# A layer with three branches: first loads, turns, gate chain and pools in another order

## The chip, the core and the metric

The kernel runs on one core of a Trainium2 chip. Its engines each work through a queue of their own in order and wait for one another by semaphores: TensorE (PE) multiplies and transposes, VectorE (DVE) and ScalarE (ACT) do arithmetic and empty PE's result banks, GpSimd (POOL) does small things, SyncE (SP) issues DMA transfers. The metric is the time on the device in microseconds, the median of the runs.

## The reference

One decoder layer on 1024 tokens of width 1024, all in float32. Here only its first part matters:

```
h    = rms_norm(x)                 # then one input projection, cut into the branches
mkv  = rms_norm(mem) @ w_kv        # memory: 256 tokens
C:   qh = rms_norm(q per head);  mk = rms_norm(k part of mkv);  mv = v part
     y2 = softmax(qh mk^T * s) @ mv
A:   mLSTM over chunks of 128 tokens, 4 heads: running maximum m of the gates,
     decays exp(i - b - m), state C carried from chunk to chunk
gates = sigmoid(h @ w_gate + b);   merge, projections, MLP
```

Branch B (differential attention), the merge and the MLP follow and are not touched.

## The kernel before

Float32 products are made of three matmuls (`mm3`, L91): each operand is split into a high part, rounded by ACT (L111 or L114), and a low part, the remainder, by DVE (L112 or L115). A weight goes by DMA into a `raw` tile, is split into a `w` tile, and the `raw` tile is free for the next load when both are done. Tiles come from pools with a number of buffers per name; a pool that closes gives its memory to the next one, and a tile that lies where an old one lay waits for that one's last reader, a store among them.

PE writes into PSUM banks: `mm` for products, two `tp` banks in turn for transposes and small products, two `sc` tiles of two banks each. A bank is taken again only when its last contents have been read.

`consts` loads a table `vraw` and `lamv`, turns the table on PE (L192) and copies it to `vec` (L194), from which scales of the rows are read. `phase_x` loads the memory rows `mx`, squares and scales them (`norm_rows`, L231 to L233), and runs `mem_kv`, a generator: turn `mx` into `memT` (L243), scaled by `vec` while it is split, then project it with three groups of weights `wkv`: the keys (copied to `kr` at L266, normalised, turned into `mkT`), then the values `mv` in two groups. Between these it loads the rows `xk` of x, normalises and turns them into `hT`.

`branch_c` puts items at places in a stream of matmuls (`weave`): at each place of the stream the items due run. A place is three matmuls. Items are `turn` (queries `cqr` into `cqT`), `scores` (with exponentials `cpe` at L380, their sum, and scalings at L387), `ptr` (turn the probabilities `cpe` into `cpT`), `values` (product with `mv` into `yc`, stored to y2).

`branch_m` does the same for the mLSTM with a stream of its own. `m_gates` (place 66) computes the gate chain, with four round trips through DRAM; `m_gates2` turns its three rows `g_b`, `g_w`, `g_a` into columns `g_col` (L559, L561). For each of eight half heads: `inter` (broadcast load `wib`, its product with the queries, split into `qp`), `krows` (keys times a column, `ks`), `decays` (broadcast load `ngb`, mask, exponentials with a column), `scores` (into a `tp` bank, times `ngb`, split into `mpT`), four `chunk`s and `final`. Gate products fill the rest of the stream (`gates`). Behind it comes a stretch of gate products alone with pools `wpg` and `rpg`.

Of the kernel before, what the change touches and what calls it, by code (L numbers as in the profile page):

```python
# [10 lines left out]
F32 = mybir.dt.float32  # L11
F32R = mybir.dt.float32r
AF = mybir.ActivationFunctionType
# [4 lines left out]
P = 128  # L18
D = 1024
S = 1024  # L20
NT = 8
# [7 lines left out]
R_SUB, R_CQ, R_CK, R_DQ, R_DK, R_END = 96, 97, 98, 99, 100, 101  # L29
# [42 lines left out]
class Layer:  # L72
# [109 lines left out]
    def consts(self, tmp):  # L182
# [6 lines left out]
        nc.vector.memset(raw, 0.0)  # L189
        nc.sync.dma_start(raw[0:R_END, :], a["vecs"])  # L190
        ps = self.tp_tile()
# [23 lines left out]
        lv = tmp.tile([P, 256], F32, name="lamv")  # L215
        nc.sync.dma_start(lv, a["lamv"].partition_broadcast(P))
        pr = tmp.tile([P, 128], F32, name="lamp")
# [18 lines left out]
    def mem_kv(self, pool, tmp, xs):  # L236
        nc, a = self.nc, self.a
        memT = tmp.tile([P, NK, 2, 256], F32R, tag="memT", name="memT")
        for k in range(0, NK, 2):
            ps = self.tp_tile()  # L240
            for i in range(2):
                for t in range(2):
                    nc.tensor.transpose(  # L243
                        ps[:, (i * 2 + t) * P : (i * 2 + t + 1) * P], xs[t][:, (k + i) * P : (k + i + 1) * P], self.ident
                    )
            for i in range(2):
                self.split(
                    memT[:, k + i, 0], memT[:, k + i, 1], ps[:, i * 256 : (i + 1) * 256],
                    self.vec[:, R_MEM + k + i : R_MEM + k + i + 1],
                )  # L250
# [10 lines left out]

        w = self.load_w(a["wkv"][0], 512, 2)
        for t in range(2):
            ps = proj(w, t)
            kr = tmp.tile([P, 512], F32, tag="kr", name=self.name("kr"))
            nc.scalar.copy(kr, ps)  # L266
            scr = tmp.tile([P, D], F32, tag="sq", name=self.name("scr"))
            nc.scalar.activation(scr[:, 0:512], ps, AF.Square)
            r4 = tmp.tile([P, 4], F32, tag="r4", name=self.name("r4"))
            nc.vector.tensor_reduce(r4, scr[:, 0:512].rearrange("p (h d) -> p h d", h=4), axis=AX.X, op=ALU.add)  # L270
            self.rsqrt_mean(r4, r4, 128, 4)
            for h in range(4):
                nc.vector.tensor_scalar_mul(kr[:, h * P : (h + 1) * P], kr[:, h * P : (h + 1) * P], r4[:, h : h + 1])
            pt = self.tp_tile()
            for h in range(4):
                nc.tensor.transpose(pt[:, h * P : (h + 1) * P], kr[:, h * P : (h + 1) * P], self.ident)
            p4 = pt.rearrange("p (h t) -> p h t", h=4)
            self.split(self.mkT[:, :, 0, t * P : (t + 1) * P], self.mkT[:, :, 1, t * P : (t + 1) * P], p4)
        for g in range(2):
            w = self.load_w(a["wkv"][1 + g], 512, 2)  # L280
            yield
            for t in range(2):
                ps = proj(w, t)
                s = slice(g * 512, (g + 1) * 512)
                self.split(self.mv[:, t, 0, s], self.mv[:, t, 1, s], ps)

    def phase_x(self, kv, tmp):
# [13 lines left out]
        mem = [load(a["mem"][t * P : (t + 1) * P, :], "mx") for t in range(2)]  # L301
        for x in mem:
            norm(x)
        gen = self.mem_kv(kv, tmp, mem)
        next(gen)
        xs = [load(a["x"][t * P : (t + 1) * P, :], "xk") for t in range(NT)]

# [22 lines left out]
    def branch_c(self, pool):  # L330
# [67 lines left out]

        def values(hf, h, v):
            c = h * 256 + v * P  # L400
            ps = self.sc_tile()[:, 0:512]
            for j in range(2):
                self.mm3(
                    ps, (self.mv[:, j, 0, c : c + P], self.mv[:, j, 1, c : c + P]),
                    (pT[hf, h, j][:, 0], pT[hf, h, j][:, 1]), j == 0, j == 1,
                )
            y = pool.tile([P, 512], F32, tag="y", name=self.name("yc"))
            if v == 0:
                nc.scalar.copy(y, ps)
            else:  # L410
                V.tensor_copy(y, ps)
            self.store_y(2, h * 2 + v, hf, y)

# [5 lines left out]
        for hf in range(2):  # L419
            for h in range(4):  # L420
                b = (43, 78)[hf] + (4, 5)[hf] * h
                add(b, ptr, hf, h, 0)
                add(b + 1, ptr, hf, h, 1)
                add(b + 5, values, hf, h, 0)
                add(b + 5, values, hf, h, 1)
        self.weave(stream(), items)
# [136 lines left out]
    def branch_m(self, pool, gp, tail):  # L563
# [262 lines left out]
        for n in range(8):  # L826
            hd, hf = heads[n // 2], n % 2
            e = Epos[n]
            late = n == 0
            kt, st, ch, fi = (9, 2, 14, 34) if n == 0 else (-2, 2, 7, 33) if n == 1 else (-16, -8, 3, 29)  # L830
# [764 lines left out]
    def run(self):  # L1595
        tc, nc = self.tc, self.nc
        with ExitStack() as ctx:
# [22 lines left out]
            with ExitStack() as c1:  # L1620
# [6 lines left out]
                with ExitStack() as c2:  # L1627
                    E2 = lambda *x, **k: c2.enter_context(tc.tile_pool(*x, **k))
                    kv = E2(name="kv", bufs=1)
                    self.wp = E2(name="wp", bufs=4)  # L1630
                    self.rp = E2(name="rp", bufs=3)
                    with tc.tile_pool(name="ptmp", bufs=1) as tmp0, tc.tile_pool(name="ptmp2", bufs=2) as tmp, tc.tile_pool(name="ptmp8", bufs=8) as tmp8:
                        class T:
                            def tile(_, shape, dt, tag, name):
                                p = tmp8 if tag == "xk" else tmp if tag in ("mx", "sq", "r1", "r4") else tmp0
# [3 lines left out]
                    with tc.tile_pool(name="pc", bufs=2) as pc, tc.tile_pool(name="pc1", bufs=1) as pc1, tc.tile_pool(name="pc3", bufs=3) as pc3, tc.tile_pool(name="pc4", bufs=6) as pc4, tc.tile_pool(name="wpc", bufs=8) as self.gwp, tc.tile_pool(name="rpc", bufs=2) as self.grp:  # L1639
                        class T2:  # L1640
# [4 lines left out]
                        self.branch_c(T2())  # L1645
                with tc.tile_pool(name="wpm", bufs=25) as self.wp, tc.tile_pool(name="rpm", bufs=3) as self.rp, tc.tile_pool(name="gm", bufs=1) as gm, tc.tile_pool(name="pm1", bufs=1) as pm1, tc.tile_pool(name="pm", bufs=2) as pm, tc.tile_pool(name="pm3", bufs=3) as pm3:
                    class T3:
# [96 lines left out]
```

## Time and profile before

| | us |
|---|---|
| median of 3 runs | 2291.28 |
| lowest, highest | 2290.56, 2292.64 |
| span of the profiled execution | 2287.7 |
| median less that span | 3.6 |
| PE busy | 2203.0 (96%) |
| DVE, ACT, POOL busy | 1388.2, 1012.3, 543.9 |

All times in the rows below are microseconds from the start of the span. "Idle before" in brackets is how long an engine had done nothing, and behind the arrow stands what released it. PEclk is TensorE's granted clock, 1.00 for 2.4 GHz and 0.50 for 1.2 GHz. The span has four parts that matter here: the loads and the memory (0 to 66 us), branch C (66 to 183), the mLSTM (183 to 561), and the rest.

### The profile page before, as it was taken

Reading aid. Unit: us, or ns where it says so; the run is one execution under the profiler, and the core shown is the slowest. Engines: PE = TensorE matmul, PEld = TensorE weight load, DVE = VectorE, ACT = ScalarE, POOL = GpSimd, SP = SyncE. Lnnn points to the kernel's source line nnn. Section 1 sums busy time; section 2 is a strip of 40 time slices with the busy share of each in tenths; the row PEclk is TensorE's granted clock in tenths of the full one; section 3 lists DMA queues with packets and bytes.
Section 4 is the critical chain, followed back from the end, with each engine's and each line's share of the span. In section 5 each row is a group of like instructions: output and inputs, shape, how many; then the busy total and the mean of one; then the engine's idle time right before and its main releaser. Section 6 shows DMA issues by size and latency. Waiting matters only on the chain.

```text
span 2287.7 us, 30578 instructions
## 1 busy us (share of the span) xinstructions
PE 2203.0 (96%) x11222; PEld 1884.3 (82%) x11222; DVE 1388.2 (61%) x2627; ACT 1012.3 (44%) x1994; POOL 543.9 (24%) x696
## 2 busy tenths in 40 slices
PE   7999999999999999999899999999999999899998
PEld 5788789888898999999787888887787888688777
DVE  6636457552147777777652123454598777856678
ACT  6533445543246666666453112223445444543332
POOL 2100000000011111111000002201576665565553
PEclk9999999999999999999999999999999999999999
DMA  6023212201311110011134225435525444844434
GB/s 242 19 79 102 88 44 83 83 24 62 98 58 33 38 37 24 19 38 33 42 113 168 101 90 174 134 115 173 195 99 204 152 153 148 319 164 152 139 128 166
DMA packets 113781, 247.90 MB, mean 108 GB/s; under 512 B 11065, under 2 KB 19550, under 8 KB 111582
## 3 DMA queue, kind: packets, MB, share of 16 engines
q1 hardware_dynamic: 111326, 233.36, 30.4%
q10 hardware_dynamic: 2304, 12.58, 1.3%
q8 instruction: 88, 1.44, 0.3%
q14 instruction: 63, 0.52, 0.1%
HBM read 178.76 MB, written 67.14 MB: 107 GB/s over the span
## 4 chain that ended last, share of the span: by engine, by line
PE 70%; DVE 14%; DMA 7%; ACT 5%; issue 3%; POOL 2%; SPq 0%; ACTq 0%; DVEq 0%; POOLq 0%
PE mm L91 43%; PE p L91 18%; PE sc L91 4%; ACT dpe L987 2%; PE po L91 2%; DVE sc L979 1%; PE tp L94 1%; DMA wraw<-in_wdown 1%; DMA raw<-in_wd 1%; DVE wo L105 1%; DVE w L112 1%; DVE dpe L1000 1%; DVE daT L112 1%; DVE dq L867 1%; DMA raw<-in_wgate 1%
## 5 line engine op out<-in xcount | busy, mean ns | idle before, releaser
L91 PE MATMUL mm<-w,hT 128*128 128x384 f32 (+3 forms) x2496 | 474.0, 331 | 13.7 <-DVE dq L867 9.0
L91 PE MATMUL mm<-hT,w 128*128 128x512 f32 x1920 | 471.0, 400 | 8.2 <-ACT w L111 5.2
L91 PEld LDWEIGHTS mm<-hT,w 128*128 128x128 f32 x1920 | 360.1, 191 | 84.9 <-ACT w L111 5.8
L91 PEld LDWEIGHTS mm<-w,hT 128*128 128x128 f32 x2496 | 387.4, 189 | 33.3 <-DVE dq L867 13.7
L91 PE MATMUL p<-xd,wo 128*128 128x512 f32 x1344 | 314.1, 395 | 16.2 <-DVE acc L1543 8.5
L91 PEld LDWEIGHTS p<-xd,wo 128*128 128x128 f32 x1344 | 253.9, 190 | 76.3 <-DVE acc L1543 12.4
L91 PE MATMUL p<-xo,wo 128*128 128x512 f32 x1344 | 307.5, 390 | 3.2 <-DVE st L1397 1.8
L91 PEld LDWEIGHTS p<-xo,wo 128*128 128x128 f32 x1344 | 251.4, 188 | 57.9 <-ACT pt L1210 2.2
L112 DVE TENSOR_TENSOR w<-raw,w 128x256 fp32r<-128x256 f32 (+3 forms) x304 | 172.9, 589 | 162.4 <-ACT w L111 161.2
L91 PE MATMUL mm<-kt,w 128*128 128x512 f32 x1152 | 261.3, 389 | 0.0
L91 PEld LDWEIGHTS mm<-kt,w 128*128 128x128 f32 x1152 | 216.2, 188 | 45.0 <-DVE w L112 0.2
L111 ACT CAST w<-raw 128x256 fp32r<-128x256 f32 (+3 forms) x304 | 154.3, 532 | 193.5 <-PE mm L91 112.8
L104 ACT CAST wo<-wraw 128x896 fp32r<-128x896 f32 x122 | 114.8, 942 | 187.7 <-PE p L91 121.9
L105 DVE TENSOR_TENSOR wo<-wraw,wo 128x896 fp32r<-128x896 f32 x122 | 146.2, 1213 | 51.3 <-ACT wo L104 51.1
L1124 POOL TENSOR_TENSOR wraw<-wraw 128x128 f32<-128x128 f32 x128 | 100.9, 788 | 207.3 <-DMA wraw<-in_wdown 132.5
L987 ACT ACTIVATE dpe<-sc,dst,drr 128x256 f32<-128x256 f32 (+7 forms) x128 | 106.6, 833 | 94.0 <-DVE dst L983 92.0
L105 DVE TENSOR_TENSOR xd<-xd 128x1536 fp32r<-128x1536 f32 (+2 forms) x36 | 69.2, 1929 | 69.4 <-ACT xd L104 69.3
L979 DVE CUSTOM_DVE_ANT_0 sc<-sc,tmask 128x256 f32<-128x256 f32 (+7 forms) x128 | 96.9, 757 | 16.5 <-PE sc L91 16.5
L1125 POOL TENSOR_TENSOR wraw<-wraw 128x128 f32<-128x128 f32 x128 | 100.9, 788 | 0.0
L127 POOL TENSOR_SCALAR drr<-drr 128x16 f32<-128x16 f32 x16 | 3.6, 222 | 397.4 <-DVE drr L935 397.4
L1126 POOL TENSOR_TENSOR wraw<-wraw 128x128 f32<-128x128 f32 x128 | 90.7, 708 | 0.0
L127 POOL TENSOR_SCALAR hss<-hss 128x4 f32<-128x4 f32 x8 | 3.3, 409 | 356.2 <-ACT mscr L747 237.6
(319 smaller groups left out, 3084.9 us busy)
## 6 DMA issues: line engine op xcount, KB each, us to landing
wraw<-in_wup SPq DMA_DIRECT2D x64, 256.0 KB, 3.1
r_d<-xts SPq DMA_DIRECT2D x16, 1024.0 KB, 4.2
wraw<-in_wdown SPq DMA_DIRECT2D x64, 256.0 KB, 2.8
xd<-r_d SPq DMA_DIRECT2D x19, 768.0 KB, 6.9
xd<-r_d SPq DMA_DIRECT2D x14, 1024.0 KB, 5.9
raw<-in_wgate SPq DMA_DIRECT2D x48, 256.0 KB, 2.8
gates<-gt SPq DMA_DIRECT2D x48, 256.0 KB, 2.0
raw<-in_wd SPq DMA_DIRECT2D x32, 384.0 KB, 3.2
```

What stands on the lines that cost most here:

```text
L91: self.pin(self.nc.tensor.matmul(out, l, r, start=start, stop=stop))
L94: self.pin(self.nc.tensor.transpose(out, x, self.ident))
L104: self.A.copy(hi, src)
L105: self.V.tensor_sub(lo, src, f32(hi))
L111: nc.scalar.copy(hi, src)
L112: nc.vector.tensor_sub(lo, src, f32(hi))
L867: V.scalar_tensor_tensor(out=qT[lo, c], in0=pt[lo], scalar=self.gd[lo], in1=f32(qT[lo, c]), op0=ALU.mult, op1=ALU.subtract)
L979: V.tensor_tensor_reduce(out=sc[:, 0:n], in0=sc[:, 0:n], in1=self.tmask[:, D - n : D], scale=1.0, scalar=-3.0e38, op0=ALU.add, op1=ALU.max ...
L987: nc.scalar.activation(pe[c][:, 0:n], sc[:, 0:n], AF.Exp, bias=t8[:, 2 + c : 3 + c], scale=rr[:, i, c : c + 1], accum_out=t8[:, 4 + c : 5 ...
L1124: G.tensor_add(r[:, 4], r[:, 0], r[:, 3])
L1125: G.tensor_sub(r[:, 5], r[:, 4], r[:, 1])
L1126: G.tensor_sub(r[:, 6], r[:, 1], r[:, 0])
```

## The change

Seven edits. (1) `lamv` and `vraw` are loaded from ACT's queue instead of SP's. (2) The memory rows are turned as they are; the reciprocal root `rm` of their mean square is worked out beside it and multiplied in when `kr`, its squares and `mv` leave the bank. The first weights are requested before the turns, four rows of x before the second group's weights and four behind; `wp` has 5 buffers for 4, `rp` 4 for 3. (3) In branch C the turns of the probabilities stand three places later and four apart, the two halves of `values` become one item with one `sc` tile, one place later; `cpT` has 4 buffers for 3. (4) In the mLSTM `m_gates2` goes from 104 to 107, and for the first half head `krows`, `decays`, `scores`, the chunks and `final` go 2 to 5 places later; `inter` stays. (5) The pools of the mLSTM open in another order. (6) The scratch memory for DMA is 1024 instead of its default, so that more is left for tiles. (7) With that the places of later pools shift.

```diff
@@ consts
-        nc.sync.dma_start(raw[0:R_END, :], a["vecs"])
+        nc.scalar.dma_start(raw[0:R_END, :], a["vecs"])
...
-        nc.sync.dma_start(lv, a["lamv"].partition_broadcast(P))
+        nc.scalar.dma_start(lv, a["lamv"].partition_broadcast(P))
@@ mem_kv
+        w = self.load_w(a["wkv"][0], 512, 2)
+        yield
...
-        w = self.load_w(a["wkv"][0], 512, 2)
+        rm = []
+        for x in xs:
+            rm.append(tmp.tile([P, 1], F32, tag="rm", name=self.name("rm")))
+            scr = tmp.tile([P, D], F32, tag="sq", name=self.name("scr"))
+            nc.scalar.activation(scr, x, AF.Square, accum_out=rm[-1])
+            self.rsqrt_mean(rm[-1], rm[-1], D, 1)
...
-            nc.scalar.copy(kr, ps)
+            nc.scalar.activation(kr, ps, AF.Copy, scale=rm[t])
...
-            nc.scalar.activation(scr[:, 0:512], ps, AF.Square)
+            nc.scalar.activation(scr[:, 0:512], ps, AF.Square, scale=rm[t])
...
-                self.split(self.mv[:, t, 0, s], self.mv[:, t, 1, s], ps)
+                self.split(self.mv[:, t, 0, s], self.mv[:, t, 1, s], ps, rm[t])
@@ phase_x
-        for x in mem:
-            norm(x)
         gen = self.mem_kv(kv, tmp, mem)
         next(gen)
-        xs = [load(a["x"][t * P : (t + 1) * P, :], "xk") for t in range(NT)]
+        xs = [load(a["x"][t * P : (t + 1) * P, :], "xk") for t in range(4)]
+        next(gen)
+        xs += [load(a["x"][t * P : (t + 1) * P, :], "xk") for t in range(4, NT)]
@@ branch_c
-        def values(hf, h, v):
+        def values(hf, h):
+            sc = self.sc_tile()
+            for v in range(2):
...
-                b = (43, 78)[hf] + (4, 5)[hf] * h
+                b = (46, 79)[hf] + 4 * h
                 add(b, ptr, hf, h, 0)
                 add(b + 1, ptr, hf, h, 1)
-                add(b + 5, values, hf, h, 0)
-                add(b + 5, values, hf, h, 1)
+                add(b + 6, values, hf, h)
@@ branch_m
-        add(96 + 8, self.m_gates2, gp)
+        add(96 + 11, self.m_gates2, gp)
...
-            kt, st, ch, fi = (9, 2, 14, 34) if n == 0 else ...
+            kt, st, ch, fi = (12, 2, 19, 39) if n == 0 else ...
...
                 add(e + 9, inter, hd, hf)
-                add(e + 9, decays, hd, hf)
-                st = 10
+                add(e + 11, decays, hd, hf)
+                st = 13
@@ pools
-   wp 4, rp 3; pc3 3;  wpm 25, rpm 3, gm 1, pm1 1, pm 2, pm3 3
+   wp 5, rp 4; pc3 4;  gm 1, pm3 3, rpm 3, wpm 25, pm1 1, pm 2
-    nc = bacc.Bacc("TRN2", target_bir_lowering=False, num_devices=1)
+    nc = bacc.Bacc("TRN2", target_bir_lowering=False, num_devices=1, dynamic_dma_scratch_size=1024)
```

PE's order in branch C around the fifth scores (`sc<-mkT,cqT`): a `tp` row is one of the four transposes of a turn, of queries (`cqr`) or probabilities (`cpe`). Before, up to the scores:

```order
L94 MATMUL tp_967<-ident,cpe_735 128x128
L94 MATMUL tp_967<-ident,cpe_802 128x128
L94 MATMUL tp_967<-ident,cpe_869 128x128
L94 MATMUL tp_967<-ident,cpe_936 128x128
L91 MATMUL mm_957<-w_643,hT 128x512 x3
L94 MATMUL tp_978<-ident,cqr_949 128x128 x4
L94 MATMUL tp_986<-ident,cpe_735 128x128
L94 MATMUL tp_986<-ident,cpe_802 128x128
L94 MATMUL tp_986<-ident,cpe_869 128x128
L94 MATMUL tp_986<-ident,cpe_936 128x128
L91 MATMUL mm_957<-w_648,hT 128x512 x6
L91 MATMUL mm_957<-w_653,hT 128x512 x3
```

and now, with the scores:

```order
L91 MATMUL mm_955<-w_636,hT 128x512 x6
L91 MATMUL mm_955<-w_641,hT 128x512 x6
L94 MATMUL tp_968<-ident,cqr_947 128x128 x4
L91 MATMUL mm_955<-w_646,hT 128x512 x6
L94 MATMUL tp_982<-ident,cpe_733 128x128
L94 MATMUL tp_982<-ident,cpe_800 128x128
L94 MATMUL tp_982<-ident,cpe_867 128x128
L94 MATMUL tp_982<-ident,cpe_934 128x128
L91 MATMUL mm_955<-w_651,hT 128x512 x3
L91 MATMUL sc_993<-mkT,cqT_973 128x256 x12
L94 MATMUL tp_1019<-ident,cpe_733 128x128
```

The first turn of probabilities (`tp_967` before, `tp_982` now) has gone behind the turn of the queries and six more matmuls, and the second (`tp_986` before, `tp_1019` now) behind the scores.

DVE's order in the gate chain of the mLSTM, from the last row that the chain itself makes (`g_c`) to the split of the first scores (`mpT`). Before:

```order
L544 TENSOR_SCALAR g_c<-g_c 32x128
L561 COPY g_col<-tp_2262 128x96
L662 TENSOR_TENSOR wib_2272<-wib_2272,cv_2098 128x512
L115 SCALAR_TENSOR_TENSOR ks_2290<-tp_2285,g_col,ks_2290 128x128
L688 TENSOR_TENSOR ngb_2278<-ngb_2278,tmaskT 128x512
L115 SCALAR_TENSOR_TENSOR qp_2275<-wib_2272,qp_2275 128x512
L115 SCALAR_TENSOR_TENSOR ks_2290<-tp_2285,g_col,ks_2290 128x128 x2
L706 TENSOR_TENSOR ngb_2278<-ngb_2278,tp_2302 128x512
L115 SCALAR_TENSOR_TENSOR ks_2290<-tp_2285,g_col,ks_2290 128x128
L112 TENSOR_TENSOR mpT_2316<-ngb_2278,mpT_2316 128x512
```

and now:

```order
L552 TENSOR_SCALAR g_c<-g_c 32x128
L670 TENSOR_TENSOR wib_2256<-wib_2256,cv_2088 128x512
L696 TENSOR_TENSOR ngb_2274<-ngb_2274,tmaskT 128x512
L115 SCALAR_TENSOR_TENSOR qp_2259<-wib_2256,qp_2259 128x512
L569 COPY g_col<-tp_2268 128x96
L115 SCALAR_TENSOR_TENSOR ks_2289<-tp_2284,g_col,ks_2289 128x128 x3
L714 TENSOR_TENSOR ngb_2274<-ngb_2274,tp_2301 128x512
L115 SCALAR_TENSOR_TENSOR ks_2289<-tp_2284,g_col,ks_2289 128x128
L112 TENSOR_TENSOR mpT_2315<-ngb_2274,mpT_2315 128x512
```

The copy of the columns, `g_col`, has gone behind the product with `wib`, the mask added to `ngb` and the low half of `qp`.

SP's order at the end of the mLSTM, from the last weight of the group of gate products that fills its stream. Before:

```order
L438 DMA raw_5350<-in_wgate 128x512
L327 DMA y<-ym_5178 128x512
L327 DMA y<-ym_5202 128x512
L469 DMA gates<-gt_5429 128x512
L469 DMA gates<-gt_5495 128x512
L469 DMA gates<-gt_5523 128x512
L438 DMA raw_5591<-in_wgate 128x512
L469 DMA gates<-gt_5555 128x512
L438 DMA raw_5599<-in_wgate 128x512
```

and now:

```order
L446 DMA raw_5340<-in_wgate 128x512
L446 DMA raw_5581<-in_wgate 128x512
L446 DMA raw_5589<-in_wgate 128x512
L334 DMA y<-ym_5168 128x512
L334 DMA y<-ym_5192 128x512
L477 DMA gates<-gt_5419 128x512
L477 DMA gates<-gt_5485 128x512
L446 DMA raw_5597<-in_wgate 128x512
L446 DMA raw_5605<-in_wgate 128x512
```

Two loads of the next group's gate weights (`raw<-in_wgate`) have come forward past the two stores of y and two of the stores of `gates`, and two more past a third.

## Rows read from the trace of the kernel before

**Rows 1.** Waits of PE, 0:600 us: line, tile, releaser, total us, times, longest.

```profile
PE tp L192 <- DMA vraw<-in_vecs: 7.2, 1, 7.2
...
PE mm L91 <- ACT w L111: 4.1, 3, 2.4
PE sc L91 <- ACT cpe L380: 3.9, 2, 2.0
PE tp L276 <- DVE kr L273: 2.2, 2, 1.2
PE tp L559 <- ACT g_b L540: 1.6, 1, 1.6
PE tp L94 <- DVE cpe L387: 1.6, 1, 1.6
PE sc L91 <- ACT mpT L111: 1.0, 1, 1.0
```

**Rows 2.** Windows: stretch, length, busy us (count) by engine, PEclk, DMA share, GB/s.

```profile
114.30:117.60 3.30, 3.30 (x11) 2.70 (x10) 1.66 (x4) 0.58 (x1) 0.00 (x0) 0.50 0.42 157
131.90:135.30 3.40, 3.40 (x17) 2.81 (x18) 2.60 (x7) 0.93 (x2) 0.00 (x0) 1.00 0.27 102
240.60:247.30 6.70, 6.70 (x24) 5.74 (x23) 2.22 (x5) 1.84 (x5) 0.00 (x0) 0.50 0.51 111
564.90:568.20 3.30, 3.30 (x9) 2.55 (x8) 1.05 (x3) 2.14 (x5) 0.00 (x0) 0.50 0.46 151
```

**Rows 3.** Timeline, 0:16 us: start, busy us, engine, line, op, tiles, count, [idle <-releaser].

```profile
10.82 1.04 ACT L111 CAST w<-raw 128x1024 fp32r<-128x1024 f32 x1
...
11.67 0.75 DVE L233 TENSOR_SCALAR mx<-mx,r 128x1024 f32<-128x1024 f32 x1 [5.81 <-POOL r L128]
...
12.34 0.28 DVE L194 COPY vec<-tp 128x128 f32<-128x128 f32 x1
...
13.55 1.22 DVE L112 TENSOR_TENSOR w<-raw,w 128x1024 fp32r<-128x1024 f32 x1
...
14.80 1.65 PE L91 MATMUL mm<-w,memT 128*128 128x512 f32 x3
```

**Rows 4.** Timeline, cross attention, 110 to 114 us, ACT and DVE.

```profile
110.41 0.61 ACT L348 ACTIVATE cscr<-mm 128x512 f32<-128x512 f32 x1
...
113.06 0.61 ACT L409 COPY yc<-sc 128x512 f32<-128x512 f32 x1
...
113.44 1.14 DVE L387 TENSOR_SCALAR cpe<-cpe,cmx 128x256 f32<-128x256 f32 x4
```

**Rows 5.** Timeline, start of the mLSTM, 182 to 184 us.

```profile
182.94 1.98 ACT L111 CAST w<-raw 128x264 fp32r<-128x264 f32 x6 [0.77 <-PE sc L91]
182.94 0.69 DVE L411 COPY yc<-sc 128x512 f32<-128x512 f32 x1 [2.69 <-PE sc L91]
...
183.40 0.39 PE L91 MATMUL mm<-w,hT 128*128 128x264 f32 x1 [0.50 <-ACT w L111]
```

**Rows 6.** DMA view, 180 to 190 us: issues, KB each, median us from issue to landing.

```profile
y<-yc SPq DMA_DIRECT2D x2, 256.0 KB, 2.0
```

**Rows 7.** Timeline, gate chain, 238 to 248 us, ACT and DVE.

```profile
238.62 0.29 ACT L540 ACTIVATE g_b<-g_b 32x128 f32<-32x128 f32 x1
...
239.37 0.26 DVE L561 COPY g_col<-tp 128x96 f32<-128x96 f32 x1 [0.69 <-PE tp L559]
...
245.08 0.69 DVE L662 TENSOR_TENSOR wib<-wib,cv 128x512 f32<-128x512 f32 x1 [5.46 <-DMA wib<-g_dwi]
...
246.59 0.68 DVE L115 SCALAR_TENSOR_TENSOR qp<-wib,qp 128x512 fp32r<-128x512 f32 x1
```

**Rows 8.** Timeline, end of the mLSTM, 507 and 560 us.

```profile
507.02 0.41 ACT L111 CAST w<-raw 128x256 fp32r<-128x256 f32 x1 [0.16 <-PE mm L91]
...
560.36 0.33 SPq L438 DMA_DIRECT2D raw<-in_wgate  x1
```

**Rows 9.** DMA view, 0 to 20 us: GB/s in 40 slices of half a microsecond.

```profile
GB/s 0 0 0 23 84 82 47 114 163 246 398 415 415 412 418 434 418 418 410 418 434 418 418 410 418 418 180 25 25 25 25 66 180 221 336 262 90 180 270 229
```

More of the change, by code (lines that the diff above doesn't have):

```diff
@@ L397, in ptr @@
             pT[hf, h, j] = t
-        def values(hf, h, v):
[L400 to L412, printed above, removed]
+        def values(hf, h):
+            sc = self.sc_tile()
+            for v in range(2):
+                c = h * 256 + v * P
+                ps = sc[:, v * 512 : v * 512 + 512]
+                for j in range(2):
+                    self.mm3(
+                        ps, (self.mv[:, j, 0, c : c + P], self.mv[:, j, 1, c : c + P]),
+                        (pT[hf, h, j][:, 0], pT[hf, h, j][:, 1]), j == 0, j == 1,
+                    )
+                y = pool.tile([P, 512], F32, tag="y", name=self.name("yc"))
+                if v == 0:
+                    nc.scalar.copy(y, ps)
+                else:
+                    V.tensor_copy(y, ps)
+                self.store_y(2, h * 2 + v, hf, y)
         items = []
@@ L829, in branch_m @@
             late = n == 0
-            kt, st, ch, fi = (9, 2, 14, 34) if n == 0 else (-2, 2, 7, 33) if n == 1 else (-16, -8, 3, 29)
+            kt, st, ch, fi = (12, 2, 19, 39) if n == 0 else (-2, 2, 7, 33) if n == 1 else (-16, -8, 3, 29)
             if n >= 1:
@@ L1629, in run @@
                     kv = E2(name="kv", bufs=1)
-                    self.wp = E2(name="wp", bufs=4)
-                    self.rp = E2(name="rp", bufs=3)
+                    self.wp = E2(name="wp", bufs=5)
+                    self.rp = E2(name="rp", bufs=4)
                     with tc.tile_pool(name="ptmp", bufs=1) as tmp0, tc.tile_pool(name="ptmp2", bufs=2) as tmp, tc.tile_pool(name="ptmp8", bufs=8) as tmp8:
@@ L1634, in tile @@
                             def tile(_, shape, dt, tag, name):
-                                p = tmp8 if tag == "xk" else tmp if tag in ("mx", "sq", "r1", "r4") else tmp0
+                                p = tmp8 if tag == "xk" else tmp if tag in ("mx", "sq", "r1", "r4", "rm") else tmp0
                                 return p.tile(shape, dt, tag=tag, name=name)
@@ L1638, in run @@
                     self.gates = self.gate_steps((1, 1, 1, 3, 6))
-                    with tc.tile_pool(name="pc", bufs=2) as pc, tc.tile_pool(name="pc1", bufs=1) as pc1, tc.tile_pool(name="pc3", bufs=3) as pc3, tc.tile_pool(name="pc4", bufs=6) as pc4, tc.tile_pool(name="wpc", bufs=8) as self.gwp, tc.tile_pool(name="rpc", bufs=2) as self.grp:
+                    with tc.tile_pool(name="pc", bufs=2) as pc, tc.tile_pool(name="pc1", bufs=1) as pc1, tc.tile_pool(name="pc3", bufs=4) as pc3, tc.tile_pool(name="pc4", bufs=6) as pc4, tc.tile_pool(name="wpc", bufs=8) as self.gwp, tc.tile_pool(name="rpc", bufs=2) as self.grp:
                         class T2:
@@ L1645, in run @@
                         self.branch_c(T2())
-                with tc.tile_pool(name="wpm", bufs=25) as self.wp, tc.tile_pool(name="rpm", bufs=3) as self.rp, tc.tile_pool(name="gm", bufs=1) as gm, tc.tile_pool(name="pm1", bufs=1) as pm1, tc.tile_pool(name="pm", bufs=2) as pm, tc.tile_pool(name="pm3", bufs=3) as pm3:
+                with tc.tile_pool(name="gm", bufs=1) as gm, tc.tile_pool(name="pm3", bufs=3) as pm3, tc.tile_pool(name="rpm", bufs=3) as self.rp, tc.tile_pool(name="wpm", bufs=25) as self.wp, tc.tile_pool(name="pm1", bufs=1) as pm1, tc.tile_pool(name="pm", bufs=2) as pm:
                     class T3:
```

## The prediction, made before the result was known

> **What bounds the kernel now.** The waits of TensorE (PE) over the first 600 us come first, then the timeline around each wait, then windows for the granted clock. PE is busy nearly all of the span, and behind the first 66 us almost nothing else sets the end, so an edit is worth what PE stands idle, plus what it loses at the lower clock level. The list of waits [rows 1] names all that the change can touch: vraw 7.2 us at the start, `kr` 2.2, `cpe` twice (1.6 for the turn behind the scaling, 3.9 in two waits of 1.96 for the exponentials), weight casts 4.1 in three (the longest 2.4, before the gate group at 563.6), `g_b` 1.6 and `mpT` 1.0. The clock adds to that: in 114.3:117.6, 240.6:247.3 and 564.9:568.2 it was 0.50, which is the 1.2 GHz level, and in each case PE had just stood idle (1.96, 1.60 and 2.44 us); behind the other 1.96 us idle it stayed 1.00 in 131.9:135.3 [rows 2]. At half clock half of the stretch is lost: 1.7, 3.4 and 1.7 us. From 575 us on the instructions and what each waits for are the same in both orders; I leave that part unchanged.
>
> **Start, 0 to 66 us.** The two scalings of `mx` (0.75 us on DVE each) and their wait on POOL's rsqrt go; the transposes need only the landing of `mx`. What then comes last for the first matmul at 14.80 is `vec` (copied at 12.34) and the first weight tile, whose second half DVE now does before `vec` [rows 3]. Cast of the weight from 10.82 for 1.04, its low half 1.22, to 13.1, then the copy of `vec` and the two halves of a memT split: first matmul near 13.9, 0.9 us earlier. The norm comes back as a scale inside evictions that exist already, so it adds no pass. The waits for `kr` (2.2) may shrink, since x 0 to 3 and five weight tiles come earlier; against it DVE is nearly full between 30 and 66 us, and its work there isn't less. Ends: 0 (DVE holds the old pace) and 5 (0.9, all 2.2, and up to 1.7 of half clock at the beginning). I take 2.2, the near end being the 0.9 that rests on rows alone: **gain 2.2**.
>
> **Cross attention, 66 to 183 us.** The first turn goes from 43 to 46, behind a further turn of queries and about 2 us of matmuls; the scaling that it waited for is done by then: the 1.6 us goes. Values with one score tile no longer take the second one, whose exponentials PE waited for twice: 3.9 us, and the half clock behind the first of them, 1.7 us. What is late next: the turns now stand so close that the turn of the next queries needs the bank of the turn before the last. The freeing of that bank stands on ACT behind copy, square and four exponentials of the scores just made (0.6 for the copy, then 2.65 from 110.41 to 113.06, begun about 1.1 us after the scores, when the product that is copied is whole), and on DVE behind a reciprocal and the four scalings (1.14) [rows 4] with 0.69 us of its own, the size of the `yc` copy [rows 5]. That is 6.6 us after the scores; PE's own work to that point is 12 transposes and 15 matmuls, 4.8 us. A new stall of 1.8 us, once (the next round misses it by a hair, so 3.6 is the bound), with or without a half clock of 1.7: the same length of idle did both in [rows 2], so 0.8. Sum 1.6 + 3.9 + 1.7 - 1.8 - 0.8: **gain 4.6**, bounds 1.5 and 6.5.
>
> **Start of the mLSTM, 183 us.** In the new pool order the weight tiles lie where the last `yc` tiles lay. The first cast (182.94 before, and PE went on at 183.40) must then wait until the last y store has landed: the `yc` copy on DVE ends 183.63, and a y store takes 2.0 us to land [rows 5, 6]. So the cast starts near 185.7 to 185.9, PE near 186.3: 2.9 us later. The fourth weight, issued when DVE has split the second tile, comes as much later, so that wait stays. The 16 small `va` casts move into the wait and cost nothing. The half clock that such an idle may bring lies mostly under the wait for that fourth weight; 0.4. **Loss 3.3**, bounds 2.4 and 4.8.
>
> **Gate chain, 238 us.** Moving the columns' transposes three places (9 matmuls, 2.1 us) ends the wait of 1.60: PE, which had come at 237.3, would come at 239.4, and the exponential ended at 238.91. But `inter` keeps its place, and so the copy of the columns, `g_col`, which DVE did at 239.37, now stands on DVE behind the product with `wib` (which began 245.08, when the broadcast had landed), the mask of `ngb` and the low half of `qp` (246.59 to 247.27) [rows 7]. It ends near 247.5. Behind it are the scales of `ks` and the exponentials of the decays, and above all PE: the scores write the bank that the columns lie in. PE reaches them at 241.5 and stands until 247.5: 6.0 us. The old idle and its half clock, 1.6 + 1.0 + 3.4 = 6.0 us, go; the new idle of 6.0 brings a half clock of its own, 0 to 3.4 us, of which I take 2.0 (nearest: 1.7 behind 2.44 us). The later chunks hide the `mpT` chain: its low half ends about 252.8, PE is there at 253.1 or later. **Loss 2.0**, bounds +0.2 and -3.6.
>
> **End of the mLSTM, 563.6 us.** The next gate group's first weights were issued only at 560.36, when the old group was done [rows 8], and PE stood idle for 2.44 us. Now two are issued behind the last split of the old group's weights (cast at 507.02, [rows 8]), some 50 us earlier, and all eight casts are done about 4 us before PE asks. Nothing else takes that stall's place, since ACT and DVE are idle there. 2.4 + 1.7: **gain 4.1**, bounds 2.4 and 4.5.
>
> The smaller scratch for DMA and the pools' other sizes only move addresses; wherever that changes a wait before 575 us it is in the terms above. Sum: 2.2 + 4.6 - 3.3 - 2.0 + 4.1 = 5.6 us. The profiled execution has a span of 2287.7, 3.6 under the median of 2291.28; taken from the median, 2285.7.
>
> **A rule that speaks against it.** vraw is 101 rows of 512 B, and on SP's queue it held PE until 7.2 us [rows 1], although nothing but lamv was ahead of it. The Trainium skill, "DMA: Bandwidth & Descriptors", section "Why a DMA increments its semaphore by 16 and not by 1", says that a transfer uses the largest number of DMA engines up to 16 that divides its outer sizes, which is one for 101 rows, and its section "Queues, rings and completion order" says that an engine takes turns between queues packet by packet. By that rule each row of vraw, now on ACT's queue, waits for a 4 KB row of the loads; no row of this trace shows two queues at this place.
>
> **Rivals.**
> First, slower: vraw is starved by the loads beside it. The mechanism: the loads move 415 GB/s as soon as they flow [rows 9], 26 on each of 16 engines, so a 4 KB piece takes 0.16 us and 101 of them 16 us; begun with the loads, at about 4 us, vraw is there near 20 us. DVE's copy of `vec` stands in front of every further weight split and of the memT splits, so the first matmul comes near 22 us instead of 14.8. Front: a loss of up to 7.5 instead of a gain of 2.2, the rest as above: -7.5 + 4.6 - 3.3 - 2.0 + 4.1 = -4.1, 2295.4, and over 2296 if the new idles bring their full half clocks. It decides from a copy of `vec` some 3.4 us later than now (15.8). For it: vraw is slow already. Against: it is now issued first of its queue, before the loads flow. Chance 0.10.
> Second, no measurable change: the front gives nothing (DVE holds the pace) and the three new idles (1.8, 3.3, 6.0) each bring a full half clock, 1.7, 1.0 and 3.4. 0 + 3.7 - 4.0 - 3.4 + 4.1 = 0.4: 2290.9. Chance 0.24.
> Third, better: DVE's queue doesn't hold PE at the scores, because the broadcast lands sooner or the scores' bank is free. Then the gate chain gains 6.0 instead of losing 2.0: 2277.7. For it: the places were moved to that end, and the idle before goes in any case; against: the rows of the new order. Chance 0.11.
> Fourth, the change doesn't do what it says: the landings, not norm or order, set the start, and every moved stall reappears at its new place: 2291. Chance 0.05.
>
> **How the numbers follow.** The forecast has 0.50. Its own bounds run from about 2281 to 2290. A difference of 0.2%, 4.6 us, is about what a measurement can tell from none: faster is under 2286.7, slower over 2295.9. Of the forecast 0.40 lies under 2286.7 and 0.10 above; the third rival is faster, the second gives 0.04 to faster and 0.20 to same, the fourth is same, the first half same, half slower, and I add 0.02 to slower for what no row shows: faster 0.55, same 0.38, slower 0.07. The range goes from 2278 to 2292; outside are the first rival and parts of the third.
>
> **What would show it.** PE's waits after: no `cpe` wait of 1.96, none of 2.44 at the gate group, none for `g_b`. New: one near 1.8 us at a turn of `cqr`, 3.3 us at the first mLSTM matmul (released by the cast, the cast by the y store), and near 6 us at the scores, released by DVE's `g_col`. Wrong would be: no wait for `g_col` (third rival), `vec` copied later than 15 us (first), or a span that moves behind 575 us.

## The result: slower, and the profile after

The changed kernel takes 2298.56 us (median of 6 runs, 2296.85 to 2301.95) against 2291.07 for the kernel before beside it: ratio 1.0042, 95% interval 1.0026 to 1.0057. The medians are 7.5 us apart; the ratio alone would make it 9.6. The forecast was 5.6 us faster, with a range up to 2292. The waits of PE over the first 600 us of the changed kernel, which answer to [rows 1] (line, tile, releaser, total us, times, longest):

```profile
PE tp L192 <- DMA vraw<-in_vecs: 15.4, 1, 15.4
PE sc L91 <- ACT yc L418: 9.1, 8, 2.4
PE tp L91 <- DVE g_col L569: 5.0, 1, 5.0
PE mm L91 <- ACT w L111: 3.8, 1, 3.8
PE tp L283 <- DVE kr L280: 2.2, 2, 1.2
PE tp L94 <- DVE cpT L112: 1.7, 1, 1.7
PE sc L94 <- DVE xk L233: 1.1, 2, 0.6
PE tp L567 <- ACT g_b L548: 1.0, 1, 1.0
```

Three of these were in the forecast: 5.0 for `g_col` (6.0 forecast), 3.8 for the first weights (3.3) and 1.7 for the bank of the turn (1.8). So was the absence of the old wait before the gate group. Two were not in its sum: 15.4 us for `vraw` in place of 7.2, and 9.1 us in eight waits for `yc`, a line that [rows 1] does not have.

The stretches with the lower clock, in the same view as [rows 2] (stretch, length, busy us and count of PE, PEld, DVE, ACT, POOL, then PEclk, DMA share, GB/s):

```profile
129.40:132.60 3.20, 3.20 (x8) 2.52 (x9) 1.04 (x4) 0.00 (x0) 0.00 (x0) 0.50 0.22 82
149.90:153.10 3.20, 3.20 (x9) 2.43 (x9) 0.69 (x1) 0.00 (x0) 0.00 (x0) 0.50 0.23 85
197.70:204.30 6.60, 6.34 (x27) 6.21 (x28) 3.69 (x10) 3.56 (x12) 0.00 (x0) 0.50 0.50 140
262.50:269.20 6.70, 6.01 (x20) 5.33 (x21) 3.23 (x8) 3.25 (x9) 0.00 (x0) 0.50 0.25 82
```

The first two stand behind two waits for `yc` of 2.44 us each, the third behind 3.79 us, the last behind 5.00.

To locate the 7.5 us, both traces are cut at PE instructions that they share, and the length of each stage is compared. The two length columns are single profiled executions, and a stage that an edit leaves alone does not always take the same time. In the runs below that leave a stage of the changed kernel as it is, the start took 74.1 to 75.5 us, cross attention 116.1 to 119.3, the start of the mLSTM 31.5 to 32.0, the gate chain 349.3 to 352.4 and the gate group 84.4, in part because the clock was at half for longer or shorter:

| stage of PE's stream (ends at) | before | after | worse by | forecast |
|---|---|---|---|---|
| start (first turn of queries) | 71.44 | 74.91 | 3.5 | -2.2 |
| cross attention (last product of `values`) | 111.46 | 119.27 | 7.8 | -4.6 |
| start of the mLSTM (first gate row, `gi`) | 27.65 | 31.74 | 4.1 | 3.3 |
| gate chain, mLSTM (last transposed row, `hS`) | 350.65 | 352.24 | 1.6 | 2.0 |
| gate group (first turn of branch B) | 88.75 | 84.43 | -4.3 | -4.1 |
| all behind it | 1633.71 | 1630.44 | -3.3 | 0 |
| sum | 2283.66 | 2293.03 | 9.4 | -5.6 |

The profiled pair differs by 9.4 us to the end of the last product and by 9.2 in the span (2287.7 and 2296.9), the medians by 7.5. Three terms came out within 0.8 us of the forecast; start and cross attention came out on the other side, 5.7 and 12.4 us off. The 1.6 us of the gate chain are inside the spread of that stage. The part behind has the same instructions and waits in both; there PE ran at half clock for 34.1 us before and for 20.5 after, and half of the difference, 6.8, is more than the 3.3 us that it gained; the rest is open.

### The profile page after: what moved, and what is told of

The parts are those of the page before. It is cut to its first block, busy times and chain, and to the rows that moved or that the text cites. A ratio compares the mean times of both kernels' runs of the same rounds, so it can differ in the third digit from the quotient of the medians.

```text
span 2296.9 us, 30571 instructions
## 1 busy us (share of the span) xinstructions
PE 2197.7 (96%) x11222; PEld 1879.6 (82%) x11222; DVE 1387.0 (60%) x2625; ACT 1011.4 (44%) x1994; POOL 543.2 (24%) x696
## 4 chain that ended last, share of the span: by engine, by line
PE 70%; DVE 11%; DMA 9%; ACT 4%; issue 3%; POOL 2%; SPq 0%; ACTq 0%; DVEq 0%; POOLq 0%
PE mm L91 41%; PE p L91 19%; PE sc L91 5%; PE po L91 2%; PE tp L94 2%; DMA raw<-in_wd 2%; DMA wraw<-in_wdown 1%; ACT dpe L995 1%; DVE w L112 1%; DVE sc L987 1%; DMA kraw<-y 1%; DVE wo L105 1%; DMA xd<-r_d 1%; PE pr L94 1%; DVE dpe L1008 1%
## 5 line engine op out<-in xcount | busy, mean ns | idle before, releaser
L91 PE MATMUL mm<-w,hT 128*128 128x384 f32 (+3 forms) x2496 | 477.1, 333 | 16.1 <-DVE dq L875 9.3
```

The costliest lines, as they stand in the source:

```text
L91: self.pin(self.nc.tensor.matmul(out, l, r, start=start, stop=stop))
```

## Experiments

My theory after the result: four separate losses, each with its own cause, which can be taken away one by one. The rival in each run is that the wait only moves on.

### vraw on SP's queue again

```diff
-        nc.scalar.dma_start(raw[0:R_END, :], a["vecs"])
+        nc.sync.dma_start(raw[0:R_END, :], a["vecs"])
-        nc.scalar.dma_start(lv, a["lamv"].partition_broadcast(P))
+        nc.sync.dma_start(lv, a["lamv"].partition_broadcast(P))
```

> The changed kernel with vraw and lamv loaded from SP's queue again, ahead of the memory rows, and nothing else. Theory: on ACT's queue vraw is starved by the loads that SP's queue issues at the same time (it landed at 15.30 us, before 7.2), and PE waits for it for 15.4 us. Back on SP's queue it lands near 7.5, PE's wait for it is near 7.5 and the first product with the memory starts near 14 us instead of 17.30; the span falls by 3 to 5 us. Rival: the loss of the beginning comes from the new order of the loads and of the norm, and the front is only shifted: the first product comes earlier but the first turn of the queries still starts near 74.9 us, and the span falls by less than 1.5 us.

2294.73 us, ratio to before 1.0022 (1.0011 to 1.0034). PE's waits over 0 to 72 us:

```profile
PE tp L192 <- DMA vraw<-in_vecs: 6.9, 1, 6.9
PE tp L283 <- DVE kr L280: 2.1, 2, 1.2
PE tp L245 <- DMA mx<-in_mem: 1.4, 2, 0.8
PE sc L94 <- DVE xk L233: 0.9, 2, 0.6
PE mm L91 <- ACT memT L114: 0.9, 1, 0.9
PE mm L91 <- DVE w L112: 0.7, 3, 0.4
```

The first product with the memory starts at 11.94 us (17.30 after, 14.80 before), the first turn of queries at 71.17 (74.91, 71.44). The queue was the whole loss of this stage. The totals alone do not part this run from the changed kernel, since the intervals overlap; the stage does. It also shows what the rest of the new beginning is worth: 2.9 us at the first product, but only 0.3 us at the turn of the queries, which is within the spread (the kernel before took 71.07 us for this stage in a later run that edits only its `values`).

### vraw on ACT's queue in two pieces

```diff
-        nc.scalar.dma_start(raw[0:R_END, :], a["vecs"])
+        nc.scalar.dma_start(raw[0:96, :], a["vecs"][0:96])
+        nc.scalar.dma_start(raw[96:R_END, :], a["vecs"][96:R_END])
```

> The changed kernel with vraw, still on ACT's queue, loaded as two transfers, 96 rows and 5 rows. Theory: the 101 rows of 512 B go through one of the 16 DMA engines, one behind the other, and on that engine each waits for a piece of the loads on SP's queue (101 pieces in about 10 us, 0.18 us apart, beside 0.025 us apart before); 96 rows divide over 16 engines, so 6 rows on each, and vraw lands within 2 to 3 us of lamv, at 6 to 9 us, and PE's wait for it falls from 15.4 to under 9. Rival: ACT's queue itself is served late while SP's queue is full, whatever the shape: vraw lands at 13 us or later.

The DMA view of the changed kernel from 7 to 15 us (packets and bytes by queue; q1 is SP's, q10 ACT's) shows the starving at work:

```profile
DMA packets 861, 2.95 MB, mean 369 GB/s; under 512 B 99, under 2 KB 147, under 8 KB 861
## 3 DMA queue, kind: packets, MB, share of 16 engines
q1 hardware_dynamic: 812, 2.92, 89.4%
q10 hardware_dynamic: 49, 0.02, 1.0%
```

In 8 us ACT's queue got 49 packets through, one every 0.16 us, although a packet took only some 0.026 us of an engine (1.0% of 16 engines for 8 us, by 49). That is the 0.16 us that the first rival of the prediction had for a piece of the loads. In two pieces PE's waits over 0 to 20 us are:

```profile
PE tp L193 <- DMA vraw<-in_vecs: 8.0, 1, 8.0
PE mm L91 <- ACT memT L114: 2.2, 1, 2.2
```

Same queue, same bytes, same loads beside it: the wait falls from 15.4 to 8.0 us, the first product starts at 12.39 and the first turn of queries at 71.63. So beside these loads it was the shape of the transfer that made it starve, and not ACT's queue by itself. A single run, without an interval: 2294.05 us.

### Both products of values ahead of their copies

```diff
                         (pT[hf, h, j][:, 0], pT[hf, h, j][:, 1]), j == 0, j == 1,
                     )
+            for v in range(2):
+                ps = sc[:, v * 512 : v * 512 + 512]
                 y = pool.tile([P, 512], F32, tag="y", name=self.name("yc"))
```

> The changed kernel with the two products of an item of values issued one behind the other and their two copies behind both. Theory: with one score tile for both, the second product waits for the first one's copy on ACT although it writes another bank, since the wait is kept for the tile; 9.1 us in 8 waits and two stretches at half clock (3.4 us) go, and no wait of the products for yc on ACT is left: the span falls by 9 to 12.5 us. Rival: the tile is what is short, and the waits only move to the next user of it (the next scores or values wait for the copies): the span falls by less than 5 us.

First the wait itself, in the timeline of the changed kernel from 128.5 to 130.4 us (start, busy us, engine, line, op, tiles, count, idle before and its releaser):

```profile
128.07 0.58 ACT L387 ACTIVATE cpe<-sc,cmx,cr 128x256 f32<-128x256 f32 x1
128.52 0.23 ACT L387 ACTIVATION_READ_ACCUMULATOR cpe<-sc,cmx,cr 128x1 f32 x1
128.62 0.61 ACT L418 COPY yc<-sc 128x512 f32<-128x512 f32 x1
...
129.28 1.65 PE L91 MATMUL sc<-cpT,mv 128*128 128x512 f32 x3 [2.44 <-ACT yc L418]
```

The second product of an item writes the other bank of the score tile (`values` takes one half of the tile for each), but it stands behind the first one's copy, and that copy stands on ACT behind the exponentials of the scores made just before. Where no exponentials are queued the wait is 0.67 to 0.72 us, the copy alone. In the kernel before, where each product had a score tile of its own, no product waits for `yc`. With both copies behind both products the median is 2290.09, ratio 0.9992 (0.9977 to 1.0006), and PE's waits from 71.2 to 200 us are:

```profile
PE mm L91 <- ACT w L111: 4.6, 1, 4.6
PE tp L94 <- DVE cpT L112: 1.7, 1, 1.7
PE mm L91 <- DVE w L112: 0.4, 1, 0.4
```

No wait for `yc` is left and none took its place in this stage; the 4.6 us are the first wait of the mLSTM, 3.8 in the changed kernel. PE's clock:

```profile
75.40:180.40 105.00, 103.27 (x541) 86.07 (x539) 48.68 (x98) 47.38 (x117) 9.17 (x15) 1.00 0.15 55
```

Cross attention takes 104.94 us: 14.3 less than after, 6.5 less than before. Where the clock did not fall, the unrepaired stage took 116.1 and 117.3 us in other runs, so 11 to 14 us are gone. The waits (9.1) and the half clock (3.4) account for 12.5 of the 14.3; the other 1.8 are open. The theory asked for 9 to 12.5 of the span; the two profiled spans are 8.2 us apart (2296.9 and 2288.7), mainly because the part behind 650 us took 5.0 us longer in this execution.

### The same values in the kernel before, at the old places

```diff
-        def values(hf, h, v):
+        def values(hf, h):
+            sc = self.sc_tile()
+            for v in range(2):
...
+            for v in range(2):
+                ps = sc[:, v * 512 : v * 512 + 512]
...
-                add(b + 5, values, hf, h, 0)
-                add(b + 5, values, hf, h, 1)
+                add(b + 5, values, hf, h)
```

> The kernel before with one change: values as one item with one score tile, both products first and both copies behind them, at the old places. Theory: the two waits of 1.96 us for the exponentials go with the second score tile alone, and a half clock with them: the stretch from the first turn of queries to the last values (111.46 us) falls by 4 to 6 us, and the wait of 1.56 for the scaled cpe stays. Rival: the gain of the cross attention needs the later places as well; at the old places the values wait for the turns instead, and the stretch falls by less than 2 us.

2282.38 us, ratio 0.9973 (0.9959 to 0.9988): faster than before with this edit alone. PE's waits from 71 to 200 us:

```profile
PE mm L91 <- ACT w L111: 2.2, 2, 1.2
PE tp L94 <- DVE cpe L387: 1.6, 1, 1.6
...
PE tp L94 <- DVE cpT L112: 0.3, 1, 0.3
```

The two waits of 1.96 us for the exponentials [rows 1] are gone, and no stretch of this stage is at half clock; it takes 105.44 us. So 6.0 of the 6.5 us come from the one score tile. The later places traded the 1.6 us wait for `cpe` against 1.7 for the bank.

### The copy of the columns first

```diff
-        self.nc.vector.tensor_copy(self.gcol, ps2[:, 0 : 3 * W])
+        self.pin(self.nc.vector.tensor_copy(self.gcol, ps2[:, 0 : 3 * W]))
-                add(e + 9, inter, hd, hf)
+                add(e + 12, inter, hd, hf)
```

A pinned instruction keeps its place in the written order of its engine; the product with `wib` and the mask of `ngb` are pinned in the same way.

> The changed kernel with inter three places later and the copy of the columns kept ahead of the mask and the product with wib in DVE's order. Theory: the scores of the first half head wait 5.0 us only because the copy stands behind two instructions that wait for DMAs; with it ahead, no wait for g_col over 0.5 us, and the half clock behind it (3.4 us) goes as well; 4.5 to 8 us less, the rest being a short wait of about 1 us for mpT. Rival: the DMA broadcasts set the end in any case (ngb landed at 261.65 us), and PE stands at the product with mpT instead, 3 us or more: the span falls by less than 3 us.

DVE around the copy in the changed kernel, to be read against [rows 7]:

```profile
260.55 0.69 DVE L670 TENSOR_TENSOR wib<-wib,cv 128x512 f32<-128x512 f32 x1 [5.03 <-DMA wib<-g_dwi]
261.67 0.69 DVE L696 TENSOR_TENSOR ngb<-ngb,tmaskT 128x512 f32<-128x512 f32 x1 [0.43 <-DMA ngb<-g_dng]
262.28 0.68 DVE L115 SCALAR_TENSOR_TENSOR qp<-wib,qp 128x512 fp32r<-128x512 f32 x1
262.88 0.25 DVE L569 COPY g_col<-tp 128x96 f32<-128x96 f32 x1
```

DVE stood idle for 5.03 us with the copy queued behind the product with `wib`. In the experiment the copy is made at 255.27 and PE does not wait for it, but 226 to 300 us reads:

```profile
PE sc L91 <- ACT mpT L111: 1.7, 1, 1.7
PE sc L91 <- ACT ks L114: 1.3, 1, 1.3
PE tp L567 <- ACT g_b L548: 0.3, 1, 0.3
PE sc L91 <- DVE ks L115: 0.2, 1, 0.2
```

5.0 us became 3.2, the half clock of 6.83 us came all the same, and the stage went from 352.24 to 350.20, only 2.0 us. An unchanged gate chain took 349.29 in another run (`vraw` in two pieces), so of these 2.0 us the stage shows nothing; the shorter waits are shown. The theory asked for 4.5 to 8: here the rival had the better number. The cause of the wait was right, but the broadcasts (`ngb` masked from 261.24) are the next bound behind it. Median 2294.65, ratio 1.0023 (1.0008 to 1.0037).

### The mLSTM's pools

Three runs. The first puts wpm and rpm behind gm and pm3 behind those, and the raw pool of the next stage first:

```diff
-   pools gm, pm3, rpm, wpm, pm1, pm; then wpg, rpg
+   pools gm, wpm, rpm, pm3, pm1, pm; then rpg, wpg
```

> The changed kernel with the pools of the mLSTM in the order gm, wpm, rpm, pm3, pm1, pm, and of the next stage's two pools the raw one first. The weights of the mLSTM then lie where no yc tile lay, and the next stage's raw tiles lie over gate tiles and not over weights that are read late. Theory: the 3.79 us wait of the first mLSTM product was a wait for the y store, since its weight tiles lie over yc: it falls to the 0.5 to 0.8 of the kernel before, and the gain at the gate group stays (no wait over 1 us there); the span falls by 2.5 to 5 us. Rival: the gain at the gate group hangs on the order with the weights behind everything, and a wait of about 2.4 us with a half clock comes back there: the span falls by less than 1 us.

The wait at the start fell to 0.50 and 1.41 us (31.74 to 29.11 for the stage), but the gate group got waits of 0.25 and 1.01 us (84.43 to 86.33), and the total did not move: ratio 1.0048 (1.0033 to 1.0064), like the changed kernel's. Neither side of the forecast fits: the wait at the gate group is just over the 1 us of the theory and under the 2.4 of the rival. The order of the pools cannot be chosen for one stage alone. The second run leaves the changed order and moves yc away:

```diff
-   {"cpe": pc4, "cpT": pc3, "cscr": pc1, "gt": pc1, "cqT": pc1}
+   {"cpe": pc4, "cpT": pc3, "cscr": pc1, "gt": pc1, "cqT": pc1, "y": pcy}
```

(`pcy` is a new pool of two buffers, the last of branch C.)

> The changed kernel with the yc tiles in a pool of their own behind the others of branch C, so that the mLSTM's weights, in the changed order of the pools, lie over none of them. Theory: the 3.79 us wait of the first mLSTM product is the landing of the y store and goes down to 0.5 or less, and the gain at the gate group stays whole, since the order of the later pools is that of the changed kernel; the stretch from the last values to the gate rows (31.74 us) falls to 27 to 28.5, the one from the last transposed row to branch B stays at 84.4. Rival: the first loads or the casts are late for another reason, and the wait only gets another releaser: 30 us or more.

In the changed kernel, from 194 us (four rows of the timeline):

```profile
194.27 0.69 DVE L420 COPY yc<-sc 128x512 f32<-128x512 f32 x1 [5.16 <-PE sc L91]
...
194.99 0.32 SPq L334 DMA_DIRECT2D y<-yc  x1
...
197.45 1.35 ACT L111 CAST w<-raw 128x264 fp32r<-128x264 f32 x4 [4.98 <-DMA y<-yc]
...
197.96 1.01 PE L91 MATMUL mm<-w,hT 128*128 128x264 f32 x2 [3.79 <-ACT w L111]
```

Copy, store, landing 2.5 us later, cast, product: the chain of the forecast. With yc elsewhere the casts begin earlier, and PE goes on at once, to wait a little later for the low halves of the weights, which DVE begins at 195.01, behind the copy of `yc` and the small `va` casts:

```profile
192.23 1.98 ACT L111 CAST w<-raw 128x264 fp32r<-128x264 f32 x6 [0.74 <-DMA gates<-gt]
```

```profile
193.04 0.28 PE L91 MATMUL mm<-w,hT 128*128 128x264 f32 x1
195.50 1.25 PE L91 MATMUL mm<-w,hT 128*128 128x264 f32 x4 [2.17 <-DVE w L112]
```

The stage takes 28.84 us, 2.9 less (27 to 28.5 expected), and the gate group keeps its 84.43. Median 2296.62, ratio 1.0037 (1.0021 to 1.0053); this interval does not part it from the changed kernel, the stage lengths do. The third run is the changed kernel with the old order of these pools:

```diff
-   pools gm, pm3, rpm, wpm, pm1, pm
+   pools wpm, rpm, gm, pm1, pm, pm3
```

> The changed kernel with the pools of the mLSTM in the old order (wpm first), and nothing else. Theory: one edit makes both the loss at 183 us and the gain at the gate group. The stretch from the last values to the gate rows goes from 31.74 back to 27.7 to 29.5 us, without a wait over 1.2 us for the first weights, and the one from the last transposed row of the mLSTM to branch B from 84.4 back to 88.5 to 89, with the wait of 2.4 us and its half clock. Rival: the early loads of the gate weights come from the other edits (the later places, the smaller scratch), and the second stretch stays at 84.4.

The stage at 183 us goes back to 27.94, the gate group to 88.69. At the gate group PE waits again:

```profile
PE mm L91 <- ACT w L111: 3.2, 3, 2.3
```

The longest of these waits is the one forecast, but the half clock did not come with it: from 569.59 to 658.27 us the granted clock is 1.00. The stage is long all the same, 3.2 us of it in these waits and 1.1 because PE was busy longer (85.53 us, 84.43 in the changed kernel); why is open. So the one edit made both the loss at 183 us (3.8 here) and the gain of 4.3; the other edits have no part in the early loads. A single run: 2293.50 us.

### All four repairs

vraw and lamv on SP's queue, copies behind both products, the pinned copy of the columns, yc in its own pool, and

```diff
-            kt, st, ch, fi = (12, 2, 19, 39) if n == 0 else ...
+            kt, st, ch, fi = (12, 2, 24, 44) if n == 0 else ...
```

> The changed kernel with the four repairs together: vraw and lamv on SP's queue, both products of values ahead of their copies, the copy of the columns ahead of the product with wib (with inter three places later), yc in a pool of its own; and the chunks and the end of the first half head five places later, to hide the 3.2 us for ks and mpT that stood in the third experiment. Theory: the four losses are separate and add up: 3.7 (start) + 13.8 (values) + 2 to 5 (gate chain) + 4 (start of the mLSTM) = 23 to 27 us below the changed kernel in the first 650 us, 11 to 15 below the kernel before: 2275 to 2280 us. Rival: they overlap, and where one wait goes the next comes up: within 5 us of the kernel before.

2273.58 us (median of 6 runs, 2269.93 to 2280.26), ratio to before 0.9945 (0.9925 to 0.9965): faster than both kernels, and a little under the 2275 to 2280 expected. From 200 to 650 us PE waits for

```profile
PE sc L91 <- ACT Ch L111: 1.1, 1, 1.1
PE sc L91 <- DVE mpT L112: 0.2, 1, 0.2
```

and the windows view of its first 650 us shows the clock and how full PE is:

```profile
0.00:650.00 650.00, 630.39 (x3487) 543.28 (x3488) 331.45 (x802) 302.90 (x743) 40.52 (x69) 1.00 0.25 84
```

PE is busy for 630.39 us of them (before 621.75, after 610.11), at full clock in the mean (0.99 and 0.98). Branch B starts at 634.65 us, against 649.95 before and 662.59 after: 27.9 us under the changed kernel, a little over the 23 to 27 expected. The stages: start 70.63, cross attention 104.91, start of the mLSTM 28.85, gate chain 345.84, gate group 84.41. The gate chain gave 6.4 us here, where the columns first had given 2.0 alone: with the later chunks the waits for `ks` and `mpT` are gone, and so is the half clock. No run has the later chunks alone, so their share is argued from the two lists of waits; but 345.84 is shorter than this stage was in any other run (349.29 at least).

## Why the prediction was wrong, step by step

**Start: the sign was wrong.** The step that failed is "then the copy of `vec` and the two halves of a memT split: first matmul near 13.9": it let vraw land as early as before, and left its starving to a rival with a chance of 0.10. With vraw back on SP's queue the first product came at 11.94, so it is the landing of vraw that the step had wrong. The rival's sign, `vec` copied later than 15 us, came (15.92). Its mechanism was right, one packet every 0.16 us, and its size too large: vraw came at 15.3 us, not 20, because half of its rows (52, since 49 come later) had passed by 7 us, before the loads took up all engines, and the first product started at 17.30, not 22. The argument against it, that vraw is issued first of its queue, was weak: it is issued second, behind lamv, and the loads start beside it. The traces agree with the two rules of the Trainium skill cited there ("DMA: Bandwidth & Descriptors", sections "Why a DMA increments its semaphore by 16 and not by 1" and "Queues, rings and completion order"): 96 rows and 5 in place of 101 took 7.4 us off the wait, and the packets came one every 0.16 us while the loads ran. The remaining part of the term, 2.2 us for norm and order, was too high by 1.9. The waits for `kr`, which it let shrink, stayed (2.2 us before and after, 2.1 in the experiment). With vraw back, the second turn of `kr` comes at 34.25 us (36.44 before), but the turn of the queries only 0.3 us earlier. About 0.5 us of that lead is order alone, since two more products with the memory now stand behind the turn of `kr`. PE was busy 32.48 of the 33 us from 39 to 72 before and 31.42 in the experiment, so 1.1 us more go as idle time, 0.8 of it in waits for `xk` and `w`. Where the rest goes I have not settled.

**Cross attention: the sign was wrong.** The step that failed is "Values with one score tile no longer take the second one": it was half of the matter. The 3.9 us for `cpe`, their half clock and the 1.6 did go, and the new wait at the turn came at 1.70 us where 1.8 were forecast, without a half clock. What I left out, and so put at nothing, is a wait that the one tile brings: the second product behind the copy of the first. It follows from the edit, which has both products and both copies of an item in turn on one tile, and could have been priced from [rows 4], where a copy takes 0.61 us and ACT's square and four exponentials 2.65: eight copies and twice the exponentials, an estimate of 10.2 us. Measured were 9.1 us in eight waits, and 3.4 lost to half clock. Without the wait the term is 6.5, the upper bound of the forecast; with it, minus 7.8. That is the upper end: the same eight waits brought less half clock in other runs, where the stage took 116.1 to 119.2 us, a loss of 4.6 and more.

**Start of the mLSTM: right.** The wait of 3.79 us for the landing of the y store, against 3.3 in the sum and 2.4 to 4.8 in its bounds. The half clock was longer than assumed (6.83 us, not some 1): 4.1 for the stage.

**Gate chain: the wait was right, its size close.** 5.00 us for `g_col` (6.0 forecast), a half clock of 6.83 us behind it as before, 1.0 for `g_b` that the forecast had at zero: 1.6 for the stage (2.0 forecast). That these two lie so near is luck: the stage took 349.3 to 352.4 us in runs that leave it alone, and 350.65 and 351.96 in two runs of the old order. The two waits add up to the 6.0 of the forecast; that the wait for `g_b` took as much off the one at the scores, because PE came later to them, is argued only.

**Gate group: right,** 4.3 (4.1 forecast), by the pool order as argued.

**Range and chances.** Both misses lie on one side, and together they cost 18.1 us against the sum. The range closed at 2292 with a rival at 2295.4 outside it; even that rival had cross attention as a gain of 4.6. The sum goes from 5.6 faster by 18.1 for the two, 0.8 - 0.4 - 0.2 for the three others and 3.3 given back behind 650 us to 9.4 slower.

## What to carry to other kernels

When two small tiles become one, list for every writer of the new tile which readers of it must be done first: a wait can be kept for the tile though the banks differ, and issuing all writers ahead of all readers takes it away. A small load that the first work needs belongs ahead of the bulk on the bulk's own queue, or in a number of rows that spreads over the DMA engines. The order of pools decides which old store or weight a new tile waits for; each change of it has to be followed to both ends of the pools' lives.

## What the runs showed of the hardware

The length of an idle does not say alone what it does to the clock, not even with the same instructions. In the cross attention of the changed kernel PE stands idle twice for 2.44 us. Of the seven runs with this order, two had 3.41 us at half clock behind each of them, three behind one of the two, and two behind neither. One of the last two is the run with wpm behind gm; its rows, to be read against the first two stretches of the changed kernel above:

```profile
130.50:133.70 3.20, 3.20 (x17) 2.63 (x17) 1.49 (x5) 0.00 (x0) 0.00 (x0) 1.00 0.23 84
148.10:151.30 3.20, 3.20 (x14) 2.63 (x15) 1.48 (x4) 0.00 (x0) 0.00 (x0) 1.00 0.22 82
```

The wait for `g_col`, 4.3 to 5.5 us in seven runs, brought 3.41 us at half clock once, 6.83 four times and 10.24 twice. A wait of 3.79 brought 6.83 in the changed kernel, and 4.6 at the same place brought only 3.41 (products first). 1.96 us did both before [rows 2], and no wait of about 0.7 brought any. With the columns first three idles of 1.28, 0.23 and 1.70 within 3 us brought 6.83, like one of 5.00; whether splitting an idle helps the clock this one run can't tell. With no idle over 1.7 us left, the whole stretch from 16 us to 650 ran at full clock (last experiment). A half clock read behind one idle in one execution is therefore no price for the next.

The part behind 650 us is the same in all kernels made from the changed one, and still it took 1625.0 us in one profiled execution and 1635.4 in another (the runs with the columns first and with the products first): half clock for 17 us in the one, 31 in the other, which at half of it explains 7 of the 10 us. Runs of one kernel spread by as much, those of the kernel before from 2279.3 to 2296.9. An edit worth 3 us is therefore seen in the length of its own stage, and hardly in the total; in the gate chain, which spreads by 3 us when nothing in it is changed, not even there.

A queue can wait for another queue's transfer, as the profile reads it: in the changed kernel SP, ahead of its loads of x, shows over 0 to 20 us

```profile
SPq L300 <- DMA vraw<-in_vecs: 7.9, 1, 7.9
SPq L300 <- DMA lamv<-in_lamv: 2.5, 1, 2.5
```

though these loads use neither vraw nor lamv. The kernel before has no such row. So the starved transfer also held back the loads of x by 7.9 us: the first four were all issued by 16.1 us, and by 9.1 with `vraw` in two pieces. What couples the two queues no run here shows.
